# Sums of weights on VectorE, sums of activations behind the first downward blocks: one change to a hybrid diffusion step on Trainium2

## The chip, the cores and the metric

The program runs on one core of one Trainium2 chip. The metric is the device time of one execution in microseconds (us). Three runs of the kernel before took 1695.55, 1696.11 and 1698.88 us; the median, 1696.11 us, is the time before. A change of less than about 0.2% can't be told from none.

The engines of the core appear in the profile as PE (TensorE, matmuls), PEld (its weight loads), DVE (VectorE), ACT (ScalarE), POOL (GpSimd) and SP (the queue from which the kernel issues its DMAs). Each works through its own instructions in order, and semaphores tie them together.

## What is computed

Two layers work on 640 tokens (128 of context, 512 of a noisy latent) of width 1024. In each a normalised, modulated input goes through three kinds of attention, an output projection and a gated residual; then comes the part that this change touches, the MLP, and after both layers a last RMSNorm. Cut to what matters:

```python
h2 = rmsnorm(x, norm2_g) * (1 + sc2) + sh2
x = x + g2 * (square(relu(h2 @ w_up)) @ w_down)     # 1024 -> 4096 -> 1024
```

All is float32. The kernel gets float32 accuracy from faster matmuls by splitting each operand into a high part (fp32r, a copy on ScalarE) and a low part (the difference, a subtraction on VectorE), and by adding three products: high by high, high by low, low by high.

## The kernel before

**Two ways of ordering.** Attention and the first upward products of a layer are put in order by a planner: every step is a task with an engine, an estimated length and a priority, and a list scheduler chooses which task goes next on which engine (`add`, and `prio` in it; a smaller number goes first). The rest of the MLP is written out by hand: one loop over blocks of matmuls, in which the order of the Python statements is the order in each engine's queue.

**The MLP.** The 4096 hidden features are 32 chunks `f` of 128, eight groups `g` of four. The first group's upward products come from the planner (`first_up`). Then, by hand: downward blocks of group 0, upward blocks of group 1, and then, for g from 1 to 7, upward blocks of group g+1 and downward blocks of group g. This document calls one such upward and downward group a round.

A downward tile is 128 x 1024 weights of w_down and serves two blocks (the first 256 tokens, then the other 384), each of two PSUM banks of four times three matmuls. VectorE adds a bank to the residual (line 747).

**The upward blocks are a Strassen-Winograd product.** Two chunks f, f+1 form a pair: a 2 x 2 arrangement of the halves of w_up's rows by the two chunks, against a 2 x 2 arrangement of halves of the activations. Seven products, in the order A11, A12, S2, S3, S1, A22, S4, take the place of eight. Each is a block of 12 matmuls of 128x320, so a group has 14 blocks, in two pairs. Three PSUM banks X, Y and Z serve a pair: S2, S1 and S4 accumulate into X, where A11 began; A22 into Z, where S3 began. After A11, S2 and S3 ScalarE copies the bank out (`pe`). After A12, S1 and A22 VectorE adds bank and copy (line 1888), then applies relu and square (line 1889); after S4 it takes relu and square straight from the bank (line 1884). ScalarE and VectorE then split the result into high and low parts (`Gt`).

The products need sums:

- **Sums of weights**, four for each pair, 128x512 each. The loads of the pair's two chunks lie in two raw tiles `wr`. As soon as the second is requested, `advance` writes two sums (into the second tile and into `ws`); the other two (`pool_late`, line 1784 and the line after it) come when the high and low parts of A12 have been made. All four are on GpSimd.
- **Sums of activations**, twelve steps (`wino_tokens`): for each of the two token ranges four sums on the kept activations `hs`, then two copies into `Th` and two subtractions into `Tl`. The planner places them, on VectorE except where it gives a copy to ScalarE.

**Rings.** Raw tiles `wr` turn in a ring of four, high and low parts `wh`, `wl` in rings of four tiles each. `prep` makes the high part of a tile on ScalarE and the low part on VectorE as soon as the block that used the tile four earlier has been written; `advance` then requests the next loads whose raw tile is free. So a load of w_up for a later group goes out when a downward tile of the current one has been split. The lines of these helpers are shared: line 401 is every copy, line 409 every subtraction, so tiles are told apart by their names.

## Time and profile before

| | |
|---|---|
| median of three runs | 1696.11 us |
| the profiled execution | 1699.22 us |
| its span, first to last instruction | 1697.4 us |
| mean granted TensorE clock | 0.986 |
| PE busy | 1612.8 us, 95% |
| VectorE busy | 1279.2 us, 75% |
| ScalarE busy | 788.3 us, 46% |
| GpSimd busy | 202.7 us, 12%, 164 instructions |
| HBM | 153 MB read, 8 MB written, 95 GB/s over the span |

The kernel is a matmul kernel with 84.6 us in which PE isn't busy. The hand-written part of layer 0 runs from about 455 to 834.5 us of the span, that of layer 1 from about 1275 to 1654.4 us. A group of the profile is named by its line, engine, operation and tiles; a line of the time line gives the start, the length, the engine, the line and the tiles, and in brackets how long the engine stood idle before and what ended that.

### The profile page before, as it was taken

The page shows a single profiled execution, that of the slowest core. Times are in us where ns is not written, and L with a number is a line of the kernel's source. Part 1 is how long each engine was busy: PE and PEld are TensorE (multiplying, and loading weights), DVE is VectorE, ACT ScalarE, POOL GpSimd, SP SyncE. Part 2 cuts the span into 40 slices and gives each one's busy share as a digit, 9 for nine tenths or more (in the row PEclk, how much of TensorE's full clock was granted, in tenths as well). Part 3 has the DMA queues.
Part 4 walks back from the last instruction along what each step waited for, and adds up shares of the span by engine and source line. Part 5 has one row for each costly group of instructions (what it writes and reads, how often), then busy time and mean ns, then how long its engine had stood idle before and what let it go on. Part 6 is the DMA issues. An engine that isn't in the chain of part 4 may idle for free.

```text
span 1697.4 us, 29299 instructions
## 1 busy us (share of the span) xinstructions
PE 1612.8 (95%) x11035; PEld 1444.5 (85%) x11035; DVE 1279.2 (75%) x3317; ACT 788.3 (46%) x1771; POOL 202.7 (12%) x164
## 2 busy tenths in 40 slices
PE   6999999998899999999999999989988999999997
PEld 4787668677899999999988766856888999999997
DVE  5875889887968666776596769999896866766666
ACT  4533777774534332343263346776463523433231
POOL 0000002000033122221000000300002322212200
PEclk9999999999899999999999999999999999999998
DMA  9433453532113212232223234124012212221121
GB/s 326 131 91 110 144 173 100 166 103 87 36 63 101 73 53 89 86 100 84 76 63 101 82 111 156 53 91 146 26 63 75 87 63 87 88 100 63 63 75 62
DMA packets 67388, 163.20 MB, mean 96 GB/s; under 512 B 6896, under 2 KB 31280, under 8 KB 67248
## 3 DMA queue, kind: packets, MB, share of 16 engines
q1 hardware_dynamic: 67248, 161.34, 29.1%
q8 instruction: 87, 1.43, 0.3%
q14 instruction: 53, 0.43, 0.1%
HBM read 153.15 MB, written 8.16 MB: 95 GB/s over the span
## 4 chain that ended last, share of the span: by engine, by line
PE 76%; DVE 14%; ACT 4%; DMA 2%; issue 2%; POOL 1%; DVEq 0%; ACTq 0%; SPq 0%; POOLq 0%
PE pu L1873 19%; PE pu L546 8%; PE pu L545 8%; PE pu L544 8%; PE po L544 3%; PE pt L1108 3%; PE O L1122 3%; PE po L546 3%; PE po L545 3%; PE pz L842 3%; PE pz L844 3%; PE pz L843 3%; PE sps L1046 1%; PE pa L578 1%; DVE wl L409 1%
## 5 line engine op out<-in xcount | busy, mean ns | idle before, releaser
L409 DVE TENSOR_TENSOR wl<-wr,wh 128x512 fp32r<-128x512 f32 (+2 forms) x290 | 293.8, 1034 | 58.4 <-ACT wh L416 30.3
L401 ACT ACTIVATE wh<-wr 128x512 fp32r<-128x512 f32 (+1 forms) x228 | 161.0, 736 | 288.8 <-PE pu L545 175.5
L546 PE MATMUL pu<-Gt,wl 128*128 128x384 f32 (+1 forms) x896 | 278.5, 311 | 5.9 <-DVE wl L409 5.9
L544 PE MATMUL pu<-Gt,wh 128*128 128x384 f32 (+1 forms) x896 | 278.3, 311 | 4.3 <-DVE r L1469 4.3
L545 PE MATMUL pu<-Gt,wh 128*128 128x384 f32 (+1 forms) x896 | 278.1, 310 | 0.0
L747 DVE SCALAR_TENSOR_TENSOR xT<-pu,ada,xT 128x128 f32<-128x128 f32 x336 | 134.1, 433 | 142.1 <-PE pu L546 142.0
L546 PEld LDWEIGHTS pu<-Gt,wl 128*128 128x128 f32 x896 | 171.7, 192 | 6.4 <-DVE wl L409 6.4
L544 PEld LDWEIGHTS pu<-Gt,wh 128*128 128x128 f32 x896 | 171.7, 192 | 4.6 <-ACT wh L416 4.6
L545 PEld LDWEIGHTS pu<-Gt,wh 128*128 128x128 f32 x896 | 171.8, 192 | 0.0
L1873 PE MATMUL pu<-Tl,wh 128*128 128x320 f32 x448 | 138.0, 308 | 0.0
L1873 PE MATMUL pu<-Th,wl 128*128 128x320 f32 x448 | 138.0, 308 | 0.0
L1873 PE MATMUL pu<-Th,wh 128*128 128x320 f32 x448 | 138.0, 308 | 0.0
L842 PE MATMUL pz<-wh,hh 128*128 128x512 f32 (+1 forms) x320 | 127.7, 399 | 3.7 <-DVE m L775 1.2
L843 PE MATMUL pz<-wl,hh 128*128 128x512 f32 (+1 forms) x320 | 122.4, 383 | 0.6 <-DVE wl L409 0.6
L844 PE MATMUL pz<-wh,hl 128*128 128x512 f32 (+1 forms) x320 | 122.8, 384 | 0.1
L1060 DVE TENSOR_REDUCE stt<-sps 128x1 f32<-128x640 f32 (+2 forms) x160 | 116.4, 736 | 7.3 <-PE sps L1053 4.2
L1068 ACT ACTIVATE quad<-sps,stt 128x640 f32<-128x640 f32 (+2 forms) x128 | 91.4, 715 | 41.1 <-DVE stt L1060 40.4
L1873 PE MATMUL pu<-hh,wh 128*128 128x320 f32 x336 | 104.2, 310 | 4.3 <-DVE r L1888 4.3
L1873 PE MATMUL pu<-hh,wl 128*128 128x320 f32 x336 | 103.8, 309 | 0.0
L1873 PE MATMUL pu<-hl,wh 128*128 128x320 f32 x336 | 103.6, 308 | 0.0
L1447 POOL TENSOR_TENSOR xT<-xT,tm 128x256 f32<-128x256 f32 (+1 forms) x32 | 33.2, 1040 | 577.8 <-ACT tm L1443 573.6
L409 POOL TENSOR_TENSOR wr<-wr 128x512 f32<-128x512 f32 x28 | 38.3, 1366 | 479.2 <-DMA wr<-in_w_up 326.0
(312 smaller groups left out, 3879.4 us busy)
## 6 DMA issues: line engine op xcount, KB each, us to landing
wr<-in_w_ada SPq DMA_DIRECT2D x80, 512.0 KB, 3.9
wr<-in_w_up SPq DMA_DIRECT2D x64, 512.0 KB, 3.4
wr<-in_w_down SPq DMA_DIRECT2D x64, 512.0 KB, 3.5
wr<-in_w_in SPq DMA_DIRECT2D x24, 512.0 KB, 3.5
wr<-in_w_out SPq DMA_DIRECT2D x16, 512.0 KB, 4.3
wq<-in_w_ada SPq DMA_DIRECT2D x6, 1024.0 KB, 11.6
wr<-in_w_in SPq DMA_DIRECT2D x8, 416.0 KB, 3.7
xT<-in_xT SPq DMA_DIRECT2D x4, 640.0 KB, 6.7
```

Source lines behind the costliest of these rows:

```text
L401: S.activation(out=out, in_=in_, func=AF.Copy)
L409: eng.tensor_tensor(out=out, in0=a, in1=b, op=ALU.subtract)
L544: T.matmul(out=out, lhsT=w[0], rhs=a[0], start=first, stop=False)
L545: T.matmul(out=out, lhsT=w[0], rhs=a[1], start=False, stop=False)
L546: T.matmul(out=out, lhsT=w[1], rhs=a[0], start=False, stop=last)
L747: V.scalar_tensor_tensor(out=xT[:, m, a:b], in0=po[:, a - a0:b - a0], scalar=ada[l][:, sec, m, s:s + 1], in1=xT[:, m, a:b], op0=ALU.mult, ...
L842: T.matmul(out=out, lhsT=h_at(h, "h", k, tk), rhs=wh[:, x], start=(k == 0), stop=False)
L843: T.matmul(out=out, lhsT=h_at(h, "h", k, tk), rhs=wl[:, x], start=False, stop=False)
L844: T.matmul(out=out, lhsT=h_at(h, "l", k, tk), rhs=wh[:, x], start=False, stop=(k == KD - 1))
L1060: add("V", tV(we) - 0.01, lambda st=st, j=j, view=view: V.tensor_reduce(out=st.t[:, j:j + 1], in_=view(), axis=AX.X if kind == "sw" else A ...
L1068: S.activation(out=out, in_=view(), func=AF.Exp, bias=st.t[:, j:j + 1], accum_out=st.t[:, 4 + j:5 + j])
L1873: T.matmul(out=out, lhsT=w_[:, k], rhs=a_[:, k], start=new and k == 0 and y == 0, stop=k == 3 and y == 2, skip_group_check=True)
```

## The change

The four sums of a pair go from GpSimd to VectorE, at the places where they were written: `pool_late` becomes `late_sums`, and the two in `advance` change their engine. The twelve steps of `wino_tokens` leave the planner: they become a list, and two of them are written behind each of the first six downward blocks. All copies into `Th` are then ScalarE's. Two priorities change: the splits of the first two w_down tiles go ahead of the last activations of `first_up`, and the second half of `first_up`'s products goes pair of chunks by pair of chunks, so that the weight buffers of the first pair come free half way.

```diff
@@ first_up
                 add("P", 3 * tP(384), mm, r=h_rd(h, k, 1) + ws[f][1], w=[] if al else [key], alloc=al,
-                    prio=1.2e6 + 1 + 0.1 * k + 0.01 * f)
+                    prio=1.2e6 + 1 + f // 2 + 0.1 * k + 0.01 * f)
@@ wino_tokens
+        steps = []
         for hf in range(2):
             a, b = HALVES[hf]
...
-                add("V", tV(w), lambda e=V, v=v, out=out, in0=in0, in1=in1: sub(
-                    e, v(*out), v(*in0), v(*in1)), r=every, w=every, prio=0.45e6 + 20)
+                steps.append(lambda v=v, out=out, in0=in0, in1=in1: sub(V, v(*out), v(*in0), v(*in1)))
             for x in (1, 0):
                 c = (slice(None), slice(4 * x, 4 * x + 4), slice(a, b))
...
-                add("AV", {"A": tA(n), "V": tV2(n)}, lambda e, c=c, sv=sv: copy(e, Th.t[c], sv()),
-                    r=src, w=[(Th, q) for q in kk], prio=0.45e6 + 20)
-                add("V", tV(n), lambda e=V, c=c, sv=sv: sub(e, Tl.t[c], sv(), Th.t[c].bitcast(F32)),
-                    r=[(Th, q) for q in kk] + src, w=[(Tl, q) for q in kk], prio=0.45e6 + 20)
+                steps.append(lambda c=c, sv=sv: copy(S, Th[c], sv))
+                steps.append(lambda c=c, sv=sv: sub(V, Tl[c], sv, Th[c].bitcast(F32)))
+        return steps
@@ the layer's plan
-            wino_tokens(hs, Tl, Th)
...
-            pre = [load_split(i["w_down"][l, 0, mc], 1024, 3.5e6 + 4 + mc, 4)[1] for mc in range(N_PRE)]
+            pre = [load_split(i["w_down"][l, 0, mc], 1024, 0.3e6 + 100 + mc, 4, load_prio=3.5e6 + 4 + mc)[1] for mc in range(N_PRE)]
@@ the hand-written part
-            def pool_late(p):
+            def late_sums(p):
                 r0 = p["r"][0]
-                G.tensor_tensor(out=r0[:, lo_], in0=p["ws"], in1=r0[:, lo_], op=ALU.add)
-                sub(G, r0[:, hi_], r0[:, hi_], p["ws"])
+                V.tensor_tensor(out=r0[:, lo_], in0=p["ws"], in1=r0[:, lo_], op=ALU.add)
+                sub(V, r0[:, hi_], r0[:, hi_], p["ws"])
...
-                            sub(G, r1[:, lo_], r0[:, lo_], r1[:, lo_])
+                            sub(V, r1[:, lo_], r0[:, lo_], r1[:, lo_])
                             p["ws"] = psum["ws"].tile([P, 512], F32, tag="ws", name="ws", bufs=RINGS["ws"])
-                            sub(G, p["ws"], r1[:, hi_], r1[:, lo_])
+                            sub(V, p["ws"], r1[:, hi_], r1[:, lo_])
...
             banks, late = {}, []
+            sums = wino_tokens([x.t for x in hs], Tlt, Tht)
...
                 late = later
+                for f_ in sums[2 * b_:2 * b_ + 2]:
+                    f_()
                 while state["tile"] < len(tiles) and last_use[state["tile"] - RINGS["wh"]] <= b_:
                     prep()
```

Two places show what this does to the order of instructions. The first is VectorE in the second pair of a settled round of layer 0, from the split of a downward tile (`wl` from `wr`, 128x1024) to the result of S4. Before:

```order
L409 TENSOR_TENSOR wl_6992<-wr_6797,wh_6991 128x1024
L1888 TENSOR_TENSOR r_7027<-pu_6936,pe_7013 128x320
L1889 SCALAR_TENSOR_TENSOR r_7027<-r_7027 128x320
L409 TENSOR_TENSOR wl_7031<-wr_6915,wh_7030 128x1024
L1888 TENSOR_TENSOR r_7048<-pu_7000,pe_6987 128x320
L1889 SCALAR_TENSOR_TENSOR r_7048<-r_7048 128x320
L409 TENSOR_TENSOR Gt_6800<-r_7027,Gt_6800 128x5x64
L1884 SCALAR_TENSOR_TENSOR r_7065<-pu_6936,r_7065 128x320
```

After the change (the lines of the file are two or three lower):

```order
L409 TENSOR_TENSOR wl_6992<-wr_6797,wh_6991 128x1024
L409 TENSOR_TENSOR wr_6995<-wr_6957,wr_6995 128x512
L409 TENSOR_TENSOR ws_6998<-wr_6995 128x512
L1886 TENSOR_TENSOR r_7027<-pu_6936,pe_7013 128x320
L1887 SCALAR_TENSOR_TENSOR r_7027<-r_7027 128x320
L409 TENSOR_TENSOR wl_7031<-wr_6915,wh_7030 128x1024
L1886 TENSOR_TENSOR r_7048<-pu_7000,pe_6987 128x320
L1887 SCALAR_TENSOR_TENSOR r_7048<-r_7048 128x320
L409 TENSOR_TENSOR Gt_6800<-r_7027,Gt_6800 128x5x64
L1882 SCALAR_TENSOR_TENSOR r_7065<-pu_6936,r_7065 128x320
```

The two sums of a pair of the next group but one (`wr_6995` and `ws_6998`) now stand between the split and S1's eviction, which reads bank `pu_6936`; S4 is accumulated into the same bank. The raw tiles `wr_6957` and `wr_6995` are the two loads that the first sum reads.

The second place is VectorE where the planner's part ends and the first downward blocks begin, in layer 0. Before, from the last of the first activations on:

```order
L409 TENSOR_TENSOR Gt_4902<-r_5509,Gt_4902 128x256
L409 TENSOR_TENSOR Tl_5058<-hs_4623,Th_5059 128x4x256
L409 TENSOR_TENSOR hs_4623<-hs_4623 128x4x3x64
...
L403 CAST Th_5059<-hs_4624 128x4x384
L409 TENSOR_TENSOR Tl_5058<-hs_4624,Th_5059 128x4x384
L409 TENSOR_TENSOR Tl_5058<-hs_4623,Th_5059 128x4x384
L1469 SCALAR_TENSOR_TENSOR r_5641<-pu_5500,r_5641 128x384
...
L409 TENSOR_TENSOR Gt_4902<-r_5650,Gt_4902 128x384
L409 TENSOR_TENSOR wl_5666<-wr_5200,wh_5635 128x1024
L409 TENSOR_TENSOR wl_5668<-wr_5271,wh_5653 128x1024
```

After the change:

```order
L409 TENSOR_TENSOR Gt_4902<-r_5517,Gt_4902 128x256
L409 TENSOR_TENSOR wl_5588<-wr_5200,wh_5576 128x1024
L409 TENSOR_TENSOR wl_5598<-wr_5271,wh_5582 128x1024
L1469 SCALAR_TENSOR_TENSOR r_5593<-pu_5499,r_5593 128x384
...
L409 TENSOR_TENSOR Gt_4902<-r_5647,Gt_4902 128x384
L409 TENSOR_TENSOR wr_5669<-wr_5667,wr_5669 128x512
L409 TENSOR_TENSOR ws_5672<-wr_5669 128x512
L409 TENSOR_TENSOR wl_5675<-wr_5663,wh_5674 128x1024
L409 TENSOR_TENSOR wl_5681<-wr_5665,wh_5680 128x1024
L409 TENSOR_TENSOR wr_5684<-wr_5678,wr_5684 128x512
L409 TENSOR_TENSOR ws_5687<-wr_5684 128x512
```

The token sums (`hs`, `Th`, `Tl`) are gone from here, the splits of the first two downward tiles stand ahead of the last activations, and the first sums of two pairs of group 1 stand ahead of the first residual additions.

## The prediction

> **What bounds the kernel now.** I read the page first, then the busy time by stretches, then who waited for whom, then the time line of one round of the MLP.

> ```profile
> span 1697.4 us, 29299 instructions
> PE 1612.8 (95%) x11035; PEld 1444.5 (85%) x11035; DVE 1279.2 (75%) x3317; ACT 788.3 (46%) x1771; POOL 202.7 (12%) x164
> 515.90:834.50 318.60, 318.60 (x2174) 318.60 (x2175) 219.91 (x389) 111.75 (x207) 62.28 (x43) 1.00 0.26 86
> 1335.90:1654.40 318.50, 318.50 (x2173) 318.50 (x2174) 219.97 (x389) 111.67 (x207) 62.64 (x43) 1.00 0.24 80
> ```

> The first two rows are the page: PE idles 84.6 us of the span. The other two are stretches (length, then PE, PEld, DVE, ACT and POOL busy, clock, DMA): the MLP of both layers once it has settled. PE has no idle time there, at full clock. VectorE is busy 69%, GpSimd 20%, and neither costs anything: in these 637 us the change can only lose time. What it can win lies where each MLP begins:

> ```profile
> PE pu L546 <- DVE wl L409: 5.7, 1, 5.7
> PE pu L544 <- DVE r L1469: 4.3, 1, 4.3
> PE pu L1873 <- DVE r L1888: 2.0, 2, 1.8
> 447.21 3.93 DVE L409 TENSOR_TENSOR hs<-hs 128x768 f32<-128x768 f32 x4
> 452.18 3.43 DVE L409 TENSOR_TENSOR Tl<-hs,Th 128x1536 fp32r<-128x1536 f32 x2
> 459.25 4.62 DVE L409 TENSOR_TENSOR wl<-wr,wh 128x1024 fp32r<-128x1024 f32 x4
> ```

> The first three rows are waits of PE in the two stretches around the beginnings (layer 0, layer 1, layer 0 again; sum, times, longest). The first downward block wants a low part of weights (wl) or the last activations (r), and VectorE is still at the token sums (hs, Th, Tl). The change moves these behind the downward blocks.

> **The sums of weights: their price.** Each pair of upward blocks takes four two-input sums of 128x512, 14 pairs in a layer, 112 sums in all. The nearest rows are those of the same form in settled rounds; a round is an upward and a downward group, 52.8 us from one start of PE's upward chain to the next:

> ```profile
> L409 DVE TENSOR_TENSOR wl<-ws,wh 128x512 fp32r<-128x512 f32 x2 | 1.4, 690 | 0.0
> L409 POOL TENSOR_TENSOR wr<-wr 128x512 f32<-128x512 f32 x2 | 2.6, 1308 | 22.4 <-DVE r L1889 17.5 <-DMA wr<-in_w_up 4.8
> 655.68 3.38 DVE L409 TENSOR_TENSOR wl<-wr,wh 128x512 fp32r<-128x512 f32 x2
> 677.07 1.29 DVE L409 TENSOR_TENSOR wl<-wr,wh 128x512 fp32r<-128x512 f32 x2 [0.21 <-ACT wh L401]
> 623.45 24.62 PE pu L1873 x168
> 676.21 24.62 PE pu L1873 x168
> ```

> A sum costs VectorE 0.69 us, about 0.63 in a row. Two such VectorE operations took 3.38 us while GpSimd worked and 1.29 without it, so with GpSimd silent VectorE also gets time back. Eight sums in a round are 5.1 us more, against the 2.1 us of this one collision given back. As throughput this is hidden behind PE and costs nothing: VectorE has 31% of 52.8, 16 us, free in a round.

> **The sums of weights: the wait they bring.** The first sum of a pair waits for the second of two loads of w_up. Before, GpSimd waited alone. In the new order the pair's two sums stand on VectorE right behind the split of a downward tile, and what follows them is the eviction L1888 of a Winograd product. One settled round, VectorE, then the issue of the load and the loads' times to landing in this stretch, then GpSimd:

> ```profile
> 642.97 1.23 DVE L409 TENSOR_TENSOR wl<-wr,wh 128x1024 fp32r<-128x1024 f32 x1 [0.46 <-ACT wh L401]
> 644.66 0.49 DVE L1888 TENSOR_TENSOR r<-pu,pe 128x320 f32<-128x320 f32 x1 [0.47 <-PE pu L1873]
> 645.19 0.49 DVE L1889 SCALAR_TENSOR_TENSOR r<-r 128x320 f32<-128x320 f32 x1
> ...
> 644.22 0.33 SPq L406 DMA_DIRECT2D wr<-in_w_up  x1
> ...
> DMA to landing us min/median/max: 3.1/3.4/4.3
> ...
> 648.05 1.30 POOL L409 TENSOR_TENSOR wr<-wr 128x512 f32<-128x512 f32 x1 [17.60 <-DVE r L1889]
> ```

> The split ends at 644.20 and thereby frees the buffer that the load wants; the load goes out at 644.22; its user starts at 648.05, 3.8 us later (the row names another releaser, but 3.8 lies within the landing times, and elsewhere the DMA is named). With the sum in VectorE's own queue nothing behind it can pass: VectorE stands from 644.20 to 648.05. Two sums take it to 649.3, and L1888 (0.49) ends at 649.8 instead of 645.15.

> Who waits for that: the 168 matmuls of the chain above are 14 products of 12, 1.76 us each. L1888 reads product S1 of the second pair, the 12th, out of a PSUM bank which the 14th, S4, accumulates into again. S4 starts at 623.45 + 13 x 1.76 = 646.3; it would have to wait until 649.8. **PE stalls 3.5 us.** This place comes five times in a layer's order (the first sums of the pairs of groups 3 to 7), ten times in all: 10 x 3.5 = 35 us. The bounds are 2.8 us a stall (a load of 3.1) and 4.0 (one of 4.3).

> The second pair of each round waits in the same way behind the last downward tile:

> ```profile
> 651.97 0.33 SPq L406 DMA_DIRECT2D wr<-in_w_up  x1
> 655.49 1.30 POOL L409 TENSOR_TENSOR wr<-wr 128x512 f32<-128x512 f32 x1 [4.63 <-DMA wr<-in_w_up]
> 669.21 0.62 DVE L747 SCALAR_TENSOR_TENSOR xT<-pu,ada,xT 128x384 f32<-128x384 f32 x1 [1.46 <-PE pu L546]
> ```

> VectorE stands another 3.5 us, but PE is then in 28.1 us of downward blocks (52.8 less 24.62) over eight PSUM banks, two to a block, so a block needs its banks back only four blocks (14 us) later. The third row shows the slack there: VectorE waits for PE 1.46 us in each such block. This wait costs nothing. If the cover were gone it would be another 3.5 us a round.

> **The clock.** A stall also may cost the clock. Stretches, fields as above:

> ```profile
> 500.00:510.00 10.00, 8.23 (x57) 7.96 (x56) 8.89 (x15) 4.78 (x10) 2.11 (x2) 1.00 0.29 107
> 1275.00:1276.00 1.00, 0.10 (x1) 0.00 (x0) 1.00 (x2) 0.98 (x3) 0.00 (x0) 1.00 0.00 0
> 1277.00:1278.00 1.00, 0.00 (x0) 0.00 (x0) 1.00 (x3) 1.00 (x4) 0.00 (x0) 0.81 0.00 0
> 1279.00:1280.00 1.00, 0.58 (x2) 0.50 (x2) 1.00 (x2) 0.69 (x2) 0.00 (x0) 0.50 0.00 0
> 1284.00:1285.00 1.00, 1.00 (x9) 1.00 (x8) 0.80 (x3) 0.00 (x0) 0.00 (x0) 0.77 0.96 352
> ```

> An idle time of 1.8 us (10 less 8.23) left the clock at 1.00. In the one of 4.3 us, which began at 1275.1, the clock fell to half after 2.3 us, at 1277.4, and came back at 1284.2; PE worked 4.8 us of that at half speed and lost 2.4. A stall of 3.5 lies between: 0 is the lower bound, 2.4 the upper. I take 1.5, nearer the longer one, since 2.3 us idle before a switching point were enough: 10 x 1.5 = 15 us.

> [...]

> **The beginning of the MLP.** Gained: the wait (5.7 us in layer 0, 4.3 in layer 1) and the half clock behind it (2.4 each, as worked out above). The split of the first two w_down tiles now stands ahead of the last activations, and the order of the first upward products by pairs of f frees their weight buffers half way. So the first downward block starts at once, 454.9 (450 and the 4.86 busy) instead of 460.5, and 28.1 us later PE is at the first upward product, 483.0 where it was 490.8:

> ```profile
> 450.00:460.00 10.00, 4.86 (x29) 4.66 (x27) 9.90 (x14) 7.74 (x13) 0.00 (x0) 0.92 0.00 0
> 460.53 0.58 PE pu L546
> 490.79 3.53 PE pu L1873 x24
> 503.11 7.32 PE pu L1873 x48
> 514.00 1.36 issue
> 473.23 1.11 DVE L747 SCALAR_TENSOR_TENSOR xT<-pu,ada,xT 128x128 f32<-128x128 f32 x4
> ```

> But VectorE has in these 28 us all that was ahead of them and the sums of weights too. From the last low part of the activations at 457.6 it runs: first pair's sums 1.3, two splits 2.3, a wait for the second pair's load 3.8, its sums 1.3 (466.3). Then eight evictions (1.11 and twice 0.6 for each two blocks, 9.2), the token pieces that stay on it (four sums 2.5, four 3.9, two low parts 2.3, two 3.4: 12.1), three pairs of splits 3.8, late sums 1.3: 492.7. PE would want the token sums for its third product at 486.5 and gets them some 4 us late. Next stand the sums of the third pair behind a load: 1.3 + 3.8 + 1.3 to 499, then 5 us until S1 is evicted: S4 starts near 504, where before it started at 503.1. The head start is used up. The fourth pair waits once more; the walk gives two further stalls of about 3 us, against the 1.36 that the old order lost there. Net +6 us a layer. The bounds: -4 (the head start of 8 kept, the old 3.2 of stalls gone, two waits of 3.5 paid) and +13 (sixteen sums, 10, and three waits, 11, all on the path, less 8). I take +6, +7 for layer 1, whose wait was 1.4 shorter.

> **The sum.** 35 + 15 + 13 = 63 us on the profiled execution's own 1699.2 gives 1762. That execution is 3.1 above the median of the three runs, 1696.11, so the forecast for the median is **1759 us**, 3.7% slower. With the bounds the addition goes from 28 - 8 = 20 to 40 + 24 + 26 = 90, or 1716 to 1786.

> **Rivals.**
> - *Stalls without the clock:* every stall as above, no half speed: 35 + 13 = 48, 1744. For it: 1.8 us idle left the clock full. Against: the drop 2.3 us into an idle time.
> - *VectorE becomes the bound of every round:* its 36 us of work, 5 of sums and 7.3 of waits are 48.7 of 52.8, but the upward half alone holds 24 us of it. If the backlog of each beginning isn't worked off in the downward half, the second wait shows as well: another 10 x 2.5, 1784. Against: the 1.46 us waits in each downward block.
> - *The other side, faster:* the load is out early enough that the sum finds its data. It decides from the place where the buffer is freed: if that were the split before (its load goes out at 640.6, data by 644.2), VectorE would not stand, the ten stalls fall away, and each beginning keeps its 8 us less 2 of added sums: 1684. For it: the sums themselves are half as long as on GpSimd. Against: the issue at 644.22 follows the split's end by 0.02 us.
> - *No change:* the stalls are a third as long (12 us) because L1888's bank is not needed so soon, and the beginnings win the 12 that the last rival gives them: 1696. Against: PE already waits for L1888, 2.0 us, where VectorE is late in the old beginning.

> **How the numbers follow.** Forecast 0.62, stalls without the clock 0.16, VectorE as the bound 0.12, faster 0.07, no change 0.03. For the range I leave out the two last and the tail above: 1728 to 1784, which the bounds on load, clock and beginning just about fill. A change under 0.2% (3.4 us) can't be told from none here. Slower by more: 0.90; within: 0.03; faster: 0.07.

> **What would show it.** In the new profile the settled stretch must have idle PE, about 3.5 us at a time, once a round, put down to L1888, which stands behind a VectorE sum that waits for the DMA of w_up; the clock column must dip in these stretches; the wait for wl at the first downward block must be gone; GpSimd must fall by 146 us or more (112 x 1.3) and VectorE rise by less than 78 (112 x 0.69), since the collisions end. If a settled round still shows 52.8 us, the forecast is wrong in its main term. If it shows 56.3 the clock held; 57.8 is my case.

## The result: 3.5% slower

| | before | after |
|---|---|---|
| median, four runs each | 1697.49 us | 1757.22 us |
| range of the runs | 1695.55 to 1699.19 | 1756.05 to 1760.96 |
| span of the profiled execution | 1697.4 us | 1754.3 us |
| mean granted TensorE clock | 0.986 | 0.976 |

The ratio of the times is 1.0345, with a 95% interval of 1.0325 to 1.0365. The forecast was 1759 us, in a range of 1728 to 1784. Two of the kernels further down had one execution each that lay far from all others (2243.9 and 3139.7 us) and is left out of their times; with it their medians would be 1706.9 and 1737.5 us in place of 1705.7 and 1735.2. The head of the page after the change:

```profile
span 1754.3 us, 29202 instructions
PE 1634.1 (93%) x11035; PEld 1462.7 (83%) x11035; DVE 1287.2 (73%) x3427; ACT 791.2 (45%) x1773; POOL 36.9 (2%) x52
```

GpSimd lost 165.8 us of work, VectorE gained only 8.0, and PE's matmuls, as many as before, take 21 us longer. VectorE's groups by form show why it gained so little, and what came with the sums (busy time and mean ns of one; then the idle time ahead of them and what ended it):

```profile
L409 DVE TENSOR_TENSOR wl<-wr,wh 128x512 fp32r<-128x512 f32 x170 | 141.3, 864 | 10.3 <-ACT wh L401 10.1
...
L409 DVE TENSOR_TENSOR wl<-wr,wh 128x512 fp32r<-128x512 f32 x170 | 110.8, 686 | 7.7 <-ACT wh L401 7.6
L409 DVE TENSOR_TENSOR wr<-wr 128x512 f32<-128x512 f32 x28 | 19.4, 692 | 96.4 <-DMA wr<-in_w_up 93.6 <-issue 2.8
```

The first row is the kernel before, the other two the changed one. The 170 low parts of halves took 864 ns each before and take 686 now. The 28 first sums cost 19.4 us of work and 96.4 us of standing, 93.6 of them for a load of w_up. The settled rounds of both layers, each in a row (length, then PE, PEld, DVE, ACT and POOL busy, clock, DMA); before, every one of them lasted 52.76 us at a clock of 1.00:

```profile
578.29:634.57 56.28, 53.02 (x363) 52.76 (x362) 37.16 (x72) 18.48 (x35) 0.00 (x0) 1.00 0.23 76
634.57:692.40 57.83, 54.57 (x363) 54.30 (x362) 37.15 (x72) 18.27 (x34) 0.00 (x0) 0.97 0.22 74
692.40:750.28 57.88, 54.56 (x363) 54.30 (x362) 37.33 (x72) 18.45 (x35) 0.00 (x0) 0.97 0.22 73
750.28:808.08 57.80, 54.55 (x362) 54.29 (x362) 37.25 (x72) 18.36 (x35) 0.00 (x0) 0.97 0.22 73
1428.40:1486.24 57.84, 54.54 (x363) 54.27 (x362) 37.38 (x72) 18.37 (x35) 0.00 (x0) 0.97 0.22 73
1486.24:1544.16 57.92, 54.52 (x363) 54.25 (x362) 37.31 (x72) 18.36 (x35) 0.00 (x0) 0.97 0.22 74
1544.16:1600.60 56.44, 53.03 (x363) 52.76 (x362) 37.16 (x72) 18.48 (x35) 0.00 (x0) 1.00 0.23 75
1600.60:1658.55 57.95, 54.42 (x363) 54.16 (x362) 37.19 (x72) 18.36 (x35) 0.00 (x0) 0.97 0.22 74
```

Two kinds of round are to be seen. Where the clock held, a round grew by 3.5 to 3.7 us; where it dipped, by 5.0 to 5.2. What stands in the first of them, as the chain of waits behind the start of S4 at 604.41 (start, length, what):

```profile
597.82 1.24 DVE wl L409
599.07 3.39 DMA wr<-in_w_up
...
602.54 0.70 DVE wr L409
603.26 0.04 DVE ws L409
...
603.87 0.49 DVE r L1886
...
604.41 2.02 PE pu L1871 x12
```

And PE's table of waits for the whole run (sum, times, longest):

```profile
PE pu L1871 <- DVE r L1886: 34.9, 12, 3.5
PE pu L1871 <- ACT pe L401: 16.3, 8, 3.7
```

That is the predicted chain link by link: the split of a downward tile, the load that the split let go, the two sums, the eviction behind them, S4. The second row of waits is new too. It lies in the beginnings of the two MLPs, where ScalarE's copies of product banks (`pe`) come late; a chain further down shows why.

So that all runs can be compared, I cut each span in three. The *settled rounds* are the four rounds of each layer shown above. The *first stretches* run, in each layer, from the first upward product of the hand-written part to the start of the first settled round; they hold the upward blocks of groups 1 and 2 and the downward blocks of group 1, and had the beginning's head start or delay to digest. The rest is the *remainder*. The first stretches before (fields as above):

```profile
490.63:570.53 79.90, 77.93 (x530) 77.40 (x530) 62.45 (x100) 32.51 (x64) 24.25 (x16) 1.00 0.24 80
1310.21:1390.49 80.28, 77.91 (x529) 77.39 (x529) 60.47 (x100) 32.52 (x64) 23.89 (x16) 1.00 0.24 80
```

And after:

```profile
480.06:578.13 98.07, 85.90 (x529) 84.18 (x529) 68.86 (x128) 34.73 (x66) 0.00 (x0) 0.91 0.21 70
1331.22:1428.24 97.02, 84.53 (x529) 82.55 (x529) 67.72 (x126) 34.74 (x66) 0.00 (x0) 0.93 0.21 71
```

The settled rounds grew by 37.9 us (459.9 against 422.1), the first stretches by 34.9 (195.1 against 160.2), and the remainder fell by 15.8 (1099.3 against 1115.1). The sum is the 56.9 us between the spans. Of the 34.9 us, 14.6 are matmuls at half clock (PE busy 170.4 us in place of 155.8) and 20.3 are idle time of PE. The remainder's gain is what the moved sums of activations bring: the first upward product of layer 0 starts at 480.06 in place of 490.63.

### The profile page after: what moved, and what is told of

It is laid out like the page before. It is cut to its first block, busy times and chain, and to the rows that moved or that the text cites. A ratio compares the mean times of both kernels' runs of the same rounds, so it can differ in the third digit from the quotient of the medians.

```text
span 1754.3 us, 29202 instructions
## 1 busy us (share of the span) xinstructions
PE 1634.1 (93%) x11035; PEld 1462.7 (83%) x11035; DVE 1287.2 (73%) x3427; ACT 791.2 (45%) x1773; POOL 36.9 (2%) x52
## 4 chain that ended last, share of the span: by engine, by line
PE 54%; DVE 10%; DMA 3%; ACT 3%; issue 2%; DVEq 0%; ACTq 0%
PE pu L1871 15%; PE pu L544 7%; PE pu L545 7%; PE pu L546 7%; DMA wr<-in_w_up 3%; PE po L544 2%; PE po L546 2%; PE po L545 2%; DVE wl L409 2%; PE O L1122 2%; PE pt L1108 2%; PE pz L842 1%; PE pz L844 1%; PE pz L843 1%; DVE wr L409 1%
## 5 line engine op out<-in xcount | busy, mean ns | idle before, releaser
L409 DVE TENSOR_TENSOR wl<-wr,wh 128x512 fp32r<-128x512 f32 (+2 forms) x290 | 255.8, 903 | 60.1 <-ACT wh L416 33.6
L544 PE MATMUL pu<-Gt,wh 128*128 128x384 f32 (+1 forms) x896 | 279.3, 312 | 1.2 <-DVE r L1469 1.2
L546 PE MATMUL pu<-Gt,wl 128*128 128x384 f32 (+1 forms) x896 | 278.6, 311 | 0.0
L401 ACT ACTIVATE wh<-wr 128x512 fp32r<-128x512 f32 (+1 forms) x228 | 160.6, 735 | 256.6 <-issue 206.8
L747 DVE SCALAR_TENSOR_TENSOR xT<-pu,ada,xT 128x128 f32<-128x128 f32 x336 | 130.9, 434 | 91.3 <-PE pu L546 91.1
L544 PEld LDWEIGHTS pu<-Gt,wh 128*128 128x128 f32 x896 | 173.0, 193 | 1.6 <-DVE r L1469 1.6
L546 PEld LDWEIGHTS pu<-Gt,wl 128*128 128x128 f32 x896 | 172.2, 192 | 0.0
L1871 PE MATMUL pu<-hh,wh 128*128 128x320 f32 x336 | 110.8, 330 | 34.9 <-DVE r L1886 34.9
L1871 PE MATMUL pu<-hl,wh 128*128 128x320 f32 x336 | 109.3, 325 | 0.0
L1871 PE MATMUL pu<-hh,wl 128*128 128x320 f32 x336 | 109.3, 325 | 0.0
L401 ACT ACTIVATE Gt<-r 128x320 fp32r<-128x320 f32 (+2 forms) x128 | 59.4, 466 | 102.2 <-DVE r L1887 91.3
L1871 PEld LDWEIGHTS pu<-Th,wh 128*128 128x128 f32 x448 | 85.2, 190 | 18.4 <-ACT pe L401 18.4
```

What stands on the lines that cost most here:

```text
L401: S.activation(out=out, in_=in_, func=AF.Copy)
L409: eng.tensor_tensor(out=out, in0=a, in1=b, op=ALU.subtract)
L544: T.matmul(out=out, lhsT=w[0], rhs=a[0], start=first, stop=False)
L546: T.matmul(out=out, lhsT=w[1], rhs=a[0], start=False, stop=last)
L747: V.scalar_tensor_tensor(out=xT[:, m, a:b], in0=po[:, a - a0:b - a0], scalar=ada[l][:, sec, m, s:s + 1], in1=xT[:, m, a:b], op0=ALU.mult, ...
L1871: T.matmul(out=out, lhsT=w_[:, k], rhs=a_[:, k], start=new and k == 0 and y == 0, stop=k == 3 and y == 2, skip_group_check=True)
```

## Experiments

The theory is that VectorE stands in its own queue for a load that has just gone out, and that what is queued behind it (S1's eviction in a settled round, evictions and splits in a beginning) comes late. Three rivals were put against it: VectorE has too much work with 112 more sums (theory 2 of the expectations); the loss comes from the moved sums of activations and the priorities (theory 3); every wait of VectorE costs, wherever it stands (theory 4). All runs, medians, with the ratio to the kernel before and its 95% interval (each against runs of the kernel before on the same chip, with medians of 1697.5 to 1699.1 us); the last three columns are us of the one profiled execution, both layers together, so they don't add up to the median:

| run | time, us | ratio | first stretches | settled rounds | remainder |
|---|---|---|---|---|---|
| before | 1697.8 | | 160.2 | 422.1 | 1115.1 |
| after | 1757.2 | 1.0345 (1.0325 to 1.0365) | 195.1 | 459.9 | 1099.3 |
| only the sums of weights moved | 1760.3 | 1.0369 (1.0348 to 1.0391) | 180.7 | 463.0 | 1111.0 |
| only the sums of activations moved | 1687.5 | 0.9943 (0.9920 to 0.9965) | 162.7 | 422.1 | 1097.4 |
| first sums back on GpSimd | 1688.3 | 0.9951 (0.9933 to 0.9969) | 160.8 | 422.1 | 1099.7 |
| first sums later, on VectorE | 1681.8 | 0.9909 (0.9894 to 0.9923) | 158.4 | 422.1 | 1099.0 |
| the same in the kernel before | 1693.6 | 0.9981 (0.9971 to 0.9990) | 157.1 | 422.1 | 1112.0 |
| later for the first pairs alone | 1705.7 | 1.0039 (1.0025 to 1.0053) | 182.0 | 422.1 | 1102.5 |
| later for the second pairs alone | 1735.2 | 1.0223 (1.0203 to 1.0243) | 171.5 | 463.6 | 1102.9 |
| later for the first pairs and in the beginnings | 1681.4 | 0.9906 (0.9891 to 0.9921) | 158.4 | 422.1 | 1101.7 |
| after, 22 matmuls in the wait | 1746.2 | 1.0279 (1.0264 to 1.0295) | 191.8 | 451.7 | 1098.2 |
| after, 15 matmuls in the wait | 1743.8 | 1.0274 (1.0259 to 1.0290) | 189.1 | 451.0 | 1101.7 |
| after, 8 matmuls in the wait | 1759.1 | 1.0363 (1.0341 to 1.0385) | 192.7 | 463.3 | 1100.0 |

### The two halves of the change, each alone

The kernel before with nothing but the engine of the four sums changed:

```diff
-                G.tensor_tensor(out=r0[:, lo_], in0=p["ws"], in1=r0[:, lo_], op=ALU.add)
-                sub(G, r0[:, hi_], r0[:, hi_], p["ws"])
+                V.tensor_tensor(out=r0[:, lo_], in0=p["ws"], in1=r0[:, lo_], op=ALU.add)
+                sub(V, r0[:, hi_], r0[:, hi_], p["ws"])
...
-                            sub(G, r1[:, lo_], r0[:, lo_], r1[:, lo_])
+                            sub(V, r1[:, lo_], r0[:, lo_], r1[:, lo_])
...
-                            sub(G, p["ws"], r1[:, hi_], r1[:, lo_])
+                            sub(V, p["ws"], r1[:, hi_], r1[:, lo_])
```

> The kernel before with nothing but the four sums of a pair named on VectorE instead of GpSimd; the sums of halves of activations and all priorities stay as they were. Theory 1: ten settled stalls of 3.3 us with 1.6 us of clock each, so 1697.5 + 49 = 1746 us, between 1735 and 1755 (the two waits of 5.7 us for the first downward block may stay or grow), settled rounds 56.3 to 57.9. Theory 3 (the loss comes from the other half of the change): 1697 us or below, rounds of 52.8.

Measured: 1760.3 us, beyond the upper end of that expectation. The stalls are there; the first settled round as a stretch:

```profile
577.36:635.56 58.20, 54.54 (x362) 54.27 (x362) 37.33 (x72) 18.38 (x34) 0.00 (x0) 0.97 0.23 73
```

PE's waits show them over the whole run, and the old wait for `wl` ahead of the first downward block beside them:

```profile
PE pu L1873 <- DVE r L1888: 35.5, 12, 3.7
...
PE pu L546 <- DVE wl L409: 5.9, 2, 5.7
```

The expectation counted ten stalls. Two of them lie in the first stretches, and these grew by 20.5 us (180.7 against 160.2), about twice what two stalls cost.

The other half alone, the changed kernel with all four sums of a pair on GpSimd:

```diff
-                V.tensor_tensor(out=r0[:, lo_], in0=p["ws"], in1=r0[:, lo_], op=ALU.add)
-                sub(V, r0[:, hi_], r0[:, hi_], p["ws"])
+                G.tensor_tensor(out=r0[:, lo_], in0=p["ws"], in1=r0[:, lo_], op=ALU.add)
+                sub(G, r0[:, hi_], r0[:, hi_], p["ws"])
...
-                            sub(V, r1[:, lo_], r0[:, lo_], r1[:, lo_])
+                            sub(G, r1[:, lo_], r0[:, lo_], r1[:, lo_])
...
-                            sub(V, p["ws"], r1[:, hi_], r1[:, lo_])
+                            sub(G, p["ws"], r1[:, hi_], r1[:, lo_])
```

> The changed kernel with all four sums of a pair back on GpSimd: only the sums of halves of activations are spread behind the first downward blocks, and the priorities are the new ones. Theory 1: no settled stall, rounds as before (52.8); the two waits of 5.7 us ahead of the first downward block are gone, and what remains is the net of the beginnings: 1685 to 1705 us. The prediction's own term for the beginnings (+13) would give 1710; that term held VectorE's waits for the first loads, which are not there with the sums on GpSimd. Theory 3 (the loss comes from here): 1740 to 1757.

Measured: 1687.5 us, 10.3 less than before. Theory 3 is out. PE's stretch around the first downward block, which before had 4.86 us of work in ten, is full, and the settled rounds are as they were:

```profile
450.00:460.00 10.00, 10.00 (x75) 10.00 (x74) 9.47 (x17) 4.91 (x8) 1.98 (x3) 1.00 0.34 107
559.79:770.83 211.04, 211.04 (x1442) 211.04 (x1442) 144.23 (x256) 73.49 (x136) 46.81 (x32) 1.00 0.24 81
```

So the change held a gain of 10 us and a loss of 70 (1757.2 less 1687.5), and the loss comes with the sums of weights.

### Which sums, and is it their work or their place?

The changed kernel with the two first sums of a pair back on GpSimd, the late ones left on VectorE:

```diff
-                            sub(V, r1[:, lo_], r0[:, lo_], r1[:, lo_])
+                            sub(G, r1[:, lo_], r0[:, lo_], r1[:, lo_])
...
-                            sub(V, p["ws"], r1[:, hi_], r1[:, lo_])
+                            sub(G, p["ws"], r1[:, hi_], r1[:, lo_])
```

> The changed kernel with only the two first sums of a pair (those issued with the loads) back on GpSimd; the late sums stay on VectorE, the sums of halves of activations stay spread behind the first blocks. Theory 1 (VectorE stands in its queue for the w_up load, with the eviction L1886 behind it): the ten stalls go with their cause, ten times the 5.1 us that a settled round with a fallen clock grew (57.85 against 52.75), so 1757 - 51 = 1706 us, between 1697 and 1712, settled rounds 52.7 to 53.0, granted clock 1.00 in them. Theory 2 (VectorE simply has too much work with 56 sums): half of the sums are gone, so about half of the loss: 1727 us, rounds near 55.2. Theory 3 (the loss comes from the sums of halves of activations and the new priorities): nothing changes, 1757.

Measured: 1688.3 us, below the expected range, and equal to the kernel with all four on GpSimd within the intervals. The late sums cost nothing on VectorE; the whole 69 us go with the first ones. The expectation was too high by 18 because I again gave the first sums the ten stalls alone; the first stretches fell further, from 195.1 to 160.8.

Then all four sums stay on VectorE, but the first two are written directly before the split of the pair's first tile instead of directly behind the request of its load:

```diff
+            def first_sums(p):
+                r0, r1 = p["r"]
+                sub(V, r1[:, lo_], r0[:, lo_], r1[:, lo_])
+                p["ws"] = psum["ws"].tile([P, 512], F32, tag="ws", name="ws", bufs=RINGS["ws"])
+                sub(V, p["ws"], r1[:, hi_], r1[:, lo_])
...
-                        if b_:
-
-                            r0, r1 = p["r"]
-                            sub(V, r1[:, lo_], r0[:, lo_], r1[:, lo_])
-                            p["ws"] = psum["ws"].tile([P, 512], F32, tag="ws", name="ws", bufs=RINGS["ws"])
-                            sub(V, p["ws"], r1[:, hi_], r1[:, lo_])
...
                     for x, (f, q) in enumerate(tiles[n_]):
                         p = pair[f]
+                        if q == "A11":
+                            first_sums(p)
```

> The changed kernel with all four sums of a pair still on VectorE, but the two first sums issued directly before the split of the pair's first tile (A11) instead of directly behind the start of the load. Theory 1 (in-order wait for the load): by then the load has long landed, so nothing waits; settled rounds 52.7 to 53.0 at a granted clock of 1.00, the group of 128x512 sums with a wait for w_up falls from 96 us of idle time to under 10; 1690 to 1710 us. Theory 2 (too much work on VectorE): as many sums stand on VectorE as before, so the loss stays: 1750 to 1760 us. Theory 3 (activations' sums and priorities): 1757.

Measured: 1681.8 us, again below the range, 75 us less than the changed kernel with the same instructions on the same engines. The group of first sums:

```profile
L409 DVE TENSOR_TENSOR wr<-wr 128x512 f32<-128x512 f32 x28 | 19.1, 683 | 0.0
```

The settled rounds, four of each layer as one stretch:

```profile
558.83:769.87 211.04, 211.04 (x1442) 211.04 (x1442) 149.86 (x288) 73.49 (x136) 0.00 (x0) 1.00 0.24 81
1372.56:1583.60 211.04, 211.04 (x1442) 211.04 (x1441) 149.77 (x288) 73.50 (x136) 0.00 (x0) 1.00 0.24 81
```

No wait for w_up is left, and PE has no idle time in 422 us. Theory 2 is out: VectorE does all 112 sums and PE doesn't notice. It was the place of the sums alone. This version is 0.9% faster than the kernel before, and 5.7 us under the one with the sums on GpSimd, though the two intervals touch.

The same placing in the kernel before (all four sums on VectorE, the first two later, sums of activations and priorities as before; the diff is the two shown above together):

> The kernel before with the four sums of a pair on VectorE, the first two directly before the split of A11; the sums of halves of activations and the priorities as before. With the sums placed so that they never wait, the engine itself shows its worth: GpSimd's collisions end (59 us of VectorE's time were given back in the changed kernel) and VectorE takes on 38 us of sums. If VectorE's time isn't on the path in the settled rounds, they stay at 52.76 us and the time is 1692 to 1699 us; if the sums on VectorE cost something of their own there, it is above 1705.

Measured: 1693.6 us, 0.1 to 0.3% faster. The settled rounds stay at 52.76, four of layer 0 as one stretch:

```profile
565.60:776.64 211.04, 211.04 (x1441) 211.04 (x1441) 149.79 (x288) 73.50 (x136) 0.00 (x0) 1.00 0.24 81
```

Moved to a place without a wait, the sums are worth 3 to 4 us, about the 0.2% that can just be told from none; moved to the place of the change, 62 us of loss: the same 112 instructions. The expectation's 38 us of sums are 56 of the 112: VectorE's busy time rose by 11.5 us (1279.2 to 1290.7), it didn't fall.

### Which of the two waits in a round costs?

A round has two waits of VectorE for a load, and the prediction charged only the first. Here the first sums come later for the first pair of each group alone, and stand where the change put them for the second:

```diff
-                        if b_:
+                        if b_ and a_ % 4 != 0:
+                            first_sums(p)
...
                     for x, (f, q) in enumerate(tiles[n_]):
                         p = pair[f]
+                        if q == "A11" and f % 4 == 0:
+                            first_sums(p)
```

> The changed kernel with the first sums deferred (to directly before the split of A11) for the first pair of each group alone; those of the second pair still stand directly behind the start of their load, and VectorE still waits about 3.5 us for them behind the last downward tile of a round. Theory 1 as predicted (the wait ahead of S1's eviction is what costs; the second wait of a round has nothing urgent behind it): settled rounds of 52.7 to 53.0 us, 1682 to 1690 us, while VectorE's idle time for w_up stays at about 48 us, half of the 96. Theory 4 (each wait of VectorE costs, wherever it stands): half of the loss stays, 1715 to 1725 us.

Measured: 1705.7 us. The settled part is as expected, the whole is not. Four rounds of layer 0, and the two first stretches:

```profile
573.09:784.13 211.04, 211.04 (x1441) 211.04 (x1441) 148.74 (x288) 73.49 (x136) 0.00 (x0) 1.00 0.25 81
480.11:573.09 92.98, 83.69 (x529) 82.77 (x529) 69.56 (x129) 34.87 (x66) 0.00 (x0) 0.91 0.22 74
1310.71:1399.69 88.98, 80.25 (x529) 78.94 (x529) 67.79 (x127) 34.75 (x66) 0.00 (x0) 0.98 0.23 78
```

VectorE's group of first sums:

```profile
L409 DVE TENSOR_TENSOR wr<-wr 128x512 f32<-128x512 f32 x28 | 19.3, 689 | 53.8 <-DMA wr<-in_w_up 53.8
```

One of them in the beginning of layer 0, from VectorE's time line:

```profile
504.60 0.69 DVE L409 TENSOR_TENSOR wr<-wr 128x512 f32<-128x512 f32 x1 [4.95 <-DMA wr<-in_w_up]
```

And the largest of PE's waits in the MLPs, from the table of the whole run:

```profile
PE pu L1875 <- ACT pe L401: 16.7, 6, 3.7
```

VectorE still stands 53.8 us for w_up. In the settled rounds that costs nothing. In the beginnings, where evictions, sums of activations and splits are all queued on VectorE, the second pair's wait costs nearly 24 us (182.0 against 158.4). The profile's chain shows one way from the wait to PE: behind the load that VectorE waits for until 504.60 come its sums and splits, and L1891 at 511.63; ScalarE, in its own order, splits that result at 512.15 (`Gt`) and only then, at 513.66, copies the bank (`pe`) for which PE has stood idle 3.27 us at 514.03.

The mirror image, later for the second pairs alone (`f % 4 == 2` in the same two conditions):

> The mirror image: deferred for the second pair of each group alone. Theory 1: the wait that costs is still there, settled rounds 56.3 to 57.9 us, 1748 to 1757 us (the beginnings may give back a few us), VectorE's idle time for w_up again halved. Theory 4: 1715 to 1725 us.

Measured: 1735.2 us; settled rounds of 57.9 as expected, 463.6 in all, but the first stretches fell from 195.1 to 171.5. The settled rounds of layer 0:

```profile
568.21:799.91 231.70, 218.22 (x1441) 217.18 (x1441) 150.40 (x288) 73.48 (x136) 0.00 (x0) 0.97 0.22 73
```

So the two pairs' waits are not alike in either part: the first pair's cost the settled rounds 41.5 us (463.6 less 422.1) and the first stretches 13, two of the ten stalls among them; the second pair's cost the settled rounds nothing and the first stretches 24. Theory 4 is out for the settled rounds. The two costs in the first stretches, 13.1 and 23.6, add up to what the changed kernel has there over the one with all sums later, 36.7 (195.1 less 158.4). Both expectations failed, by 16 and 13 us beyond their ranges, because I had charged neither pair for the beginnings.

To close this, the second pair's sums come later in the beginnings as well (upward blocks up to f = 11) and stay behind their load in the settled rounds:

```diff
-                        if b_ and a_ % 4 != 0:
+                        if b_ and a_ % 4 and a_ >= 12:
                             first_sums(p)
...
-                        if q == "A11" and f % 4 == 0:
+                        if q == "A11" and (f % 4 == 0 or f < 12):
                             first_sums(p)
```

> As the kernel that defers the first pair's sums alone (1706.9 us), but for the loads of the first groups (upward blocks 4 to 11) the second pair's sums are deferred too. What is left of the waits for a load are those behind the last downward tile of the settled rounds. If those cost nothing, as the prediction had it, and the 25 us by which that kernel missed 1682 lie in the beginnings of the two MLPs (its first stretches last 93.0 and 89.0 us against 79.6 and 78.8 with all sums deferred), it takes 1682 to 1686 us with settled rounds of 52.76. If the settled wait does cost something that the rounds don't show, it stays above 1695.

Measured: 1681.4 us, as fast as with all of them later, though VectorE still stands 36 us for the loads. The group of first sums:

```profile
L409 DVE TENSOR_TENSOR wr<-wr 128x512 f32<-128x512 f32 x28 | 19.2, 686 | 36.2 <-DMA wr<-in_w_up 36.2
```

One of these waits from VectorE's time line:

```profile
594.57 0.69 DVE L409 TENSOR_TENSOR wr<-wr 128x512 f32<-128x512 f32 x1 [3.63 <-DMA wr<-in_w_up]
```

And the four settled rounds of layer 0 around it:

```profile
563.06:774.10 211.04, 211.04 (x1441) 211.04 (x1441) 148.63 (x288) 73.50 (x136) 0.00 (x0) 1.00 0.25 81
```

### Is the clock a cost of its own?

To leave the wait and take away only PE's idleness, matmuls are put ahead of the waiting block; they go to a PSUM bank of their own that nobody reads. With 22:

```diff
+                    if q == "S4" and f % 4 == 2 and 2 <= f // 4 <= 6:
+                        spare = bank()[:, 0:320].rearrange("p (t n) -> p t n", n=64)
+                        for y in range(22):
+                            T.matmul(out=spare, lhsT=whv[:, y % 4], rhs=bh[:, y % 4], start=y == 0,
+                                     stop=y == 22 - 1, skip_group_check=True)
                     for k in range(4):
```

> The changed kernel with 22 matmuls more ahead of the block that waits (S4 of the second pair, in the five groups of a layer that stall), written to a PSUM bank that nobody reads: 22 at the 0.147 us from start to start of the upward matmuls in the changed kernel's timeline are 3.2 us, nearly the whole wait. The wait of VectorE and of S4 stays as it is; TensorE only isn't idle in it. Theory 1a (the stall costs its wait, and the clock behind it is a cost of its own that comes from TensorE being idle): the clock stays at 1.00 in the settled rounds, they last 56.3 to 56.5 us in place of 57.85, and the time falls by eight to ten times 1.5 us to 1742 to 1746 us. Theory 1b (the 1.5 us beyond the wait come from something else, such as work that piled up behind the wait on VectorE): rounds stay at 57.8 and the time at 1757 us.

With 8, and with 15, in the place of 22:

> The same with 8 matmuls, 1.2 us of the wait, so that TensorE idles for some 2.1 us in place of 3.3. If a wait must be about as long as 3.3 us for the clock to fall, it stays at 1.00 and the time is that of the 22: 1742 to 1746 us. If 2.1 us are enough, the clock falls as before and the time stays at 1757 us; in between if it depends on where the wait falls.

> The changed kernel with 15 matmuls of filling (2.2 us), between the 22 that kept the clock and the 8 that didn't: TensorE idles for some 1.2 us in each settled round. If the clock falls by how much of a short stretch (the half-speed stretches last 3.4 us) is idle, 1.2 us may be little enough: rounds of 56.4 us, 1742 to 1748 us. If any idle time of a microsecond brings it down, rounds of 57.9 us and 1757 us.

Measured: 1746.2 us with 22, 1743.8 with 15, 1759.1 with 8. The four settled rounds of layer 0 as one stretch, with 22:

```profile
575.99:801.91 225.92, 225.02 (x1530) 223.97 (x1530) 148.50 (x288) 73.92 (x136) 0.00 (x0) 1.00 0.22 75
```

With 15:

```profile
576.39:801.75 225.36, 220.90 (x1502) 219.85 (x1501) 148.63 (x288) 73.93 (x136) 0.00 (x0) 1.00 0.22 76
```

One start of S4 there, from PE's time line, with the idle time ahead of it:

```profile
659.11 0.42 PE L1876 MATMUL pu<-hh,wh 128*128 128x320 f32 x1 [1.15 <-DVE r L1891]
```

The same two with 8, first the rounds:

```profile
574.60:806.16 231.56, 222.80 (x1473) 221.75 (x1473) 149.62 (x288) 73.47 (x136) 0.00 (x0) 0.97 0.21 73
```

Then the start of S4:

```profile
658.88 0.42 PE L1876 MATMUL pu<-hh,wh 128*128 128x320 f32 x1 [2.19 <-DVE r L1891]
```

With 22 and with 15 PE does 110 and 75 matmuls of filling in a layer and the time falls, by 11 and 13 us: the clock stays at 1.00 in all eight settled rounds, and these take 451.7 and 451.0 us against 459.9 (most of the rest of the fall lies in the first stretches). Theory 1a holds: the stall has two prices, its own length and the clock after it. With 8 the clock dips in all eight rounds (57.85 to 58.01 us each), although PE idles a third less than without filling, and nothing is won.

## Why the prediction was right

- **The place and the cause** were right. Each settled round has one stall of S4, behind L1886, behind the two first sums, behind the load that the split of a downward tile lets go. Putting the sums elsewhere on the same engine takes the whole loss away.
- **The length of a stall**, 3.5 us with bounds of 2.8 and 4.0: PE's idle time is 3.25 to 3.53, the round grows by 3.5 to 3.7 where the clock holds. Right.
- **The clock**, 1.5 us a stall: where it dips, a round takes 57.8 to 57.95 us in place of 56.3 to 56.4, so a dip costs 1.5; it dipped in six of the eight. That makes 1.1 a stall on average, and 37.9 / 8 = 4.7 us a round in place of 5.0. The size is right with some luck: the 1.5 was chosen between 0 and 2.4, by the reasoning that the length of the idle time decides between 1.8 and 4.3 us, and that reasoning was not right (below). The working also reads the drop in the idle time of 4.3 us as 2.3 us after its start; the mean clock of 0.81 from 1277 to 1278 puts it at 1277.6, 2.5 us after.
- **The second wait of a round costs nothing.** Right in the settled rounds. The step said that of every round, and the runs showed its limit: in the beginnings the second pair's wait costs 24 us.
- **The sums as throughput cost nothing.** Right: GpSimd fell by 165.8 us (at least 146 were forecast), VectorE rose by 8.0 (under 78). The 112 sums are about 77 us of VectorE's work at 0.68 to 0.69 each, and most of it comes back from operations that took longer while GpSimd was busy. Of the 198 low parts of 128x512 in the trace of before, 170 from `wr` and 28 from `ws`, the 47 that overlap a GpSimd instruction took 1.40 us on average and the other 151 took 0.69. The 170 alone returned 30.5 us (141.3 to 110.8, 864 to 686 ns each); they take 686 ns too in the kernel before with the sums later on VectorE, and 832 to 836 in the changed kernel with the first sums, or all four, on GpSimd. Another 3.3 us are the copies into `Th` that ScalarE took over.
- **The beginnings**, +13 for both: mis-sized. The first stretches grew by 34.9; less two of the ten stalls at 4.7 they grew by 25.5. The remainder fell by 15.8. The net is +9.7 in place of 13. The head start was forecast as 7.8 us in layer 0 (first upward product at 483.0 instead of 490.8) and came as 10.6. The term had no half clock in it beyond that of the ten stalls, and in the first stretches half clock made 14.6 us, that of two of these stalls included. The runs also show what the net hides, a gain of 17.9 us in the span, by the kernel with the sums later, nearly all of it in the remainder, and in the changed kernel the waits for the loads, which eat it and more.
- **The sum.** The working's 63 us stand against 56.9 between the two profiled executions (1699.22 and 1756.05 us) and 59.7 between the medians. Ten stalls at 4.7 and 9.7 for the beginnings make up the 56.7, by construction, as the 9.7 is what the stalls leave. That the forecast for the median came within 2 us is partly luck: the terms for the clock and the beginnings were too large together by some 6 us on the profiled executions and 3 on the medians, and the base, 1696.11, was 1.4 us below the median of four runs.
- **The rivals.** The faster one had named its condition, that the first sum finds its data there, and a time for it, 1684 us; the kernel with the sums later meets the condition and takes 1681.8. Stalls without the clock come out at 1744, the kernels with filling at 1743.8 and 1746.2, though these were not free of other shifts: their first stretches fell by 3 to 6 us too. VectorE as the bound of every round asked for another 2.5 us a round from the second wait; the settled rounds last 57.95 us at most, and they stay at 52.76 with all sums on VectorE and the second wait left in. *No change* fell with stalls of full length.

Where I was wrong was in the expectations: five of the runs ended 5 to 16 us outside the range given (two more by less than 1 us), each of the five times because only the ten stalls were counted while the runs also changed what VectorE waits for in the beginnings.

## What to carry to other kernels

VectorE works its queue off in order in these traces: in the changed kernel it stood 93.6 us for loads of w_up, with evictions waiting behind the sums. So an instruction that waits for a transfer must be written where its data has landed, not where the transfer is requested: the same sums on the same engine cost 62 us in one place and gained 3 to 4 in another. When work moves from an idle engine to a busy one, ask first what it waits for, then what is queued behind it and who waits for that; its own duration may matter least. A short stall of TensorE may cost more than its length (stalls of 3.25 to 3.53 us made settled rounds 5.0 to 5.2 us longer where the clock dipped), and the same wait may be free in one stage and dear in the next (the second pair's cost nothing in the settled rounds and 24 us in the beginnings), so the price has to be taken stage by stage.

## What the runs showed of the hardware

**How long TensorE idled didn't by itself tell whether the clock fell.** Three starts of S4 in PE's time line of the changed kernel, after 3.25, 3.40 and 3.41 us of idle time:

```profile
604.41 0.41 PE L1871 MATMUL pu<-hh,wh 128*128 128x320 f32 x1 [3.25 <-DVE r L1886]
...
1512.51 0.41 PE L1871 MATMUL pu<-hh,wh 128*128 128x320 f32 x1 [3.40 <-DVE r L1886]
...
1570.44 0.41 PE L1871 MATMUL pu<-hh,wh 128*128 128x320 f32 x1 [3.41 <-DVE r L1886]
```

The clock stayed at 1.00 in the rounds of the first and the third, and fell in that of the second. With eight matmuls of filling PE idled 2.15 to 2.28 us, and the clock fell in all eight rounds. There it fell after PE was at work again: S4 started at 658.88, and the clock was at half from 659.98 to 663.39.

```profile
599.29:602.70 3.41, 1.87 (x13) 1.60 (x11) 0.16 (x1) 1.06 (x1) 0.00 (x0) 1.00 0.48 154
602.70:606.12 3.42, 1.71 (x11) 1.71 (x12) 3.35 (x6) 0.47 (x1) 0.00 (x0) 1.00 0.01 2
606.12:609.53 3.41, 3.41 (x30) 3.41 (x29) 3.09 (x6) 2.22 (x4) 0.00 (x0) 1.00 0.53 159
...
1507.24:1510.65 3.41, 1.87 (x13) 1.60 (x11) 0.01 (x1) 1.06 (x1) 0.00 (x0) 1.00 0.44 154
1510.65:1514.06 3.41, 1.55 (x10) 1.55 (x11) 3.34 (x6) 0.47 (x1) 0.00 (x0) 1.00 0.02 5
1514.06:1517.48 3.42, 3.42 (x18) 3.42 (x17) 2.97 (x7) 2.10 (x4) 0.00 (x0) 0.50 0.44 153
```

The grid splits the first stall into 1.54 and 1.71 us of idle PE, and the clock stays; it splits the second into 1.54 and 1.86, and the next step runs at half. With 8 matmuls of filling the whole 2.2 us lie in one step:

```profile
656.56:659.98 3.42, 1.24 (x8) 1.10 (x8) 2.90 (x5) 0.47 (x1) 0.00 (x0) 1.00 0.00 0
659.98:663.39 3.41, 3.41 (x17) 3.41 (x16) 2.69 (x6) 1.74 (x4) 0.00 (x0) 0.50 0.46 157
```

Over the MLPs of all thirteen traces, from the first upward product to the last downward one, each of the 60 steps at full clock in which PE idled 1.86 us or more (11 of them in the changed kernel, none in the kernel before) was followed by one at half, and none of the 2958 with 1.77 us or less; no step lay between. So a step needn't be idle as a whole: 1.86 us of its 3.41 were enough. The 1.1 to 1.2 us that 15 matmuls leave stay below that. In other parts of the program the clock also fell after steps with less idle time (1.10 us in the step from 1236.67 to 1240.08 of the kernel before), so the bound is shown for the MLPs only. Which of these stalls lost the clock is thus a matter of where they fell: in the first stretch of layer 1 the kernel with 8 idled 2.26 us up to 1398.38, the grid split that at 1397.26 into 1.14 and 1.12, and the clock stayed. Its settled rounds of 57.9 us are nearly 17 steps (58.0), so that each stall falls where the last one did; eight dips in eight rounds aren't eight separate trials.
